# Token projections in spans of 512 tokens, queries with channels on partitions, row factors through memory

## The chip, the core and the metric

The kernel runs on one core of a Trainium2 chip. The metric is the device time of one execution in microseconds, the median of three runs. The engines are named as the profile names them: PE (matrix multiply) with PEld (its weight loads), DVE (vector), ACT (scalar), POOL (GpSimd) and SP, whose queue issues most transfers.

## The reference

One layer of a streaming encoder: 4096 prompt tokens and 32 sample tokens of 1024 channels. A row norm and one input projection of 3072 columns give queries, keys and values (512 each), a gate, a pooling input and its gate; then differential attention, trailing means, an output projection. The first sixteen channels of every 64 of a query or key are rotated by their position. Cut to what matters here:

```python
h = rmsnorm(x, norm_g)
proj = jnp.einsum('bsd,de->bse', h, w_in)
q, k, v, ga, u, gp = jnp.split(proj, [ATTN_WIDTH, 2 * ATTN_WIDTH, 3 * ATTN_WIDTH,
                                      4 * ATTN_WIDTH, 4 * ATTN_WIDTH + POOL_WIDTH], axis=-1)
q = rope(q.reshape(B, S, N_HEADS, 2, HEAD_DIM), pos)
k = rope(k.reshape(B, S, N_HEADS, 2, HEAD_DIM), pos)
k_rows, v_rows = k.reshape(B, S, N_HEADS, 128), v.reshape(B, S, N_HEADS, 128)    # outputs too
o = diff_attention(q, k_all.reshape(B, Lk, N_HEADS, 2, HEAD_DIM), v_all, pos, kpos_all, lam)
o = rmsnorm(o, subln_g, SUBLN_EPS) * (1.0 - lam_init)
a_out = o.reshape(B, S, ATTN_WIDTH) * jax.nn.silu(ga)
p_out = pool_mix(u, pool_hist, pos, w_pool, pool_scale) * jax.nn.silu(gp)
y = x + jnp.einsum('bse,ed->bsd', jnp.concatenate([a_out, p_out], axis=-1), w_out)
```

## The kernel before

The kernel has four stages: a token phase (queries, keys, values), a channel phase (gates and pooling), attention for four heads, and the output projection. Every product of the first two is made in three passes of rounded 32-bit numbers (`mm3`, L112 to L114): the high part of one operand with the high and the low part of the other, and its low part with the high part. A contraction over 1024 channels has eight chunks, so a sum takes 24 matmuls. `split` (L108, L109) makes the two parts: a rounded copy on ACT, the remainder on DVE.

The token phase goes over 33 blocks of 128 tokens (the last has 32). A block's transposed input is the stationary operand, and the weights, 1536 columns in two loads of 768, are the moving one. Four pieces of 512, 256, 256 and 512 columns fill three sums of 512: queries, keys, values. `evacuate` (L233, L235, L238) scales a row by the factor that `norms` has made of that token's norm (its square sum is L210); `rotate` turns queries and keys on POOL; `transposes` brings both across with eight PE transposes (L259), splits them and stores them in `q_scr` and `k_scr`, from which attention loads them. PE does a block's transposes after the next block's query sum.

The channel phase goes over nine spans (seven of 512 tokens, one of 256, one of 288), with the weights stationary and up to 512 tokens moving. `span_in` needs a token's factor in every partition: it multiplies an identity by the factors (`dg`, L349), and PE multiplies that by ones (`bps`, L350). `order` runs twelve sums a span; the last two spans' second halves are done in the attention phase.

A scheduler orders the instructions of each engine; each engine and each transfer queue works its list in order. Pools that bear on the change: `mid` (16 tiles of 4 KB a partition: split inputs, weights being converted), `st` (4: inputs as loaded), `sm` (8 of 2 KB: what comes out of a sum until its store has landed), `two` (three tiles of PSUM, each two banks, for the sums) and `one`, with a single bank for `tp`.

Of the kernel before, what the change touches and what calls it, by code (L numbers as in the profile page):

```python
# [30 lines left out]
LAM_INIT = 0.2  # L31
WINDOWS = (2, 4, 8, 16)
# [13 lines left out]
AFTER = {1: 12, 2: 15}  # L46
CSA = 7
# [21 lines left out]
def encoder(tc, a, o):  # L69
# [4 lines left out]
    with ExitStack() as es:  # L74
# [11 lines left out]
        q_scr = dram.tile([NH, 2, 2, 64, TOK], F32R, name="q_scr")  # L86
# [38 lines left out]
        latest, stages = [None], []  # L125
# [5 lines left out]
        def load_w(src, cols, scale, slot):  # L131

            width = sum(c1 - c0 for c0, c1 in cols)
            w = []
            for k in range(NK):
                if k % 2 == 0:
                    t = b_tile(slot + k // 2, [P, 2, 2, 768], "w")
                w.append((t[:, k % 2, 0], t[:, k % 2, 1]))
                stg = m_tile([P, 768], name="wst")
                stages.append(stg)  # L140
                x = 0
                for c0, c1 in cols:
                    dma(stg[:, x:x + c1 - c0], src[k * P:(k + 1) * P, c0:c1])
                    x += c1 - c0
                hi, lo = w[k][0][:, :width], w[k][1][:, :width]
                S.activation(hi, stg[:, :width], AF.Copy, scale=scale[:, k:k + 1])  # L146
                V.scalar_tensor_tensor(lo, stg[:, :width], scale[:, k:k + 1], hi.bitcast(F32),  # L147
                                       op0=ALU.mult, op1=ALU.subtract)
            return w
# [8 lines left out]
        ones = const.tile([P, P], F32, name="ones")  # L158
        rx = const.tile([P, NB + 1], F32, name="rx")
        rxq = const.tile([P, NB + 1], F32, name="rxq")  # L160
# [26 lines left out]


        def token_phase():

            pieces = [(0, 0, 512, 0, 0), (0, 512, 768, 1, 0), (1, 0, 256, 1, 256), (1, 256, 768, 2, 0)]

            def block_in(b):
                t0, m = b * P, (P if b < NB else DEC)
                xt = st.tile([P, NK, P], F32, tag="st", name="xt")
                if b in AFTER:
                    pace(xt[0:1, 0, 0:1], stages[AFTER[b]][0:1, 0:1])
                dma(xt[:, :, :m], a["xT"][:, t0:t0 + m].rearrange("(k p) t -> p k t", p=P))
                src = xt[:, :, :m]
                xh = m_tile([P, NK, P], F32R, name="xh")  # L200
                xl = m_tile([P, NK, P], F32R, name="xl")
                split(xh[:, :, :m], xl[:, :, :m], src)
                return [b, t0, m, xh, xl, None, [None] * 3]

            def norms(blk):
                b, t0, m = blk[:3]
                xn = m_tile([P, D], name="xn")
                dma(xn[:m], a["xn"][t0:t0 + m, :])
                junk = s_tile([P, D], BF16, name="junk")
                S.activation(junk[:m], xn[:m], AF.Square, accum_out=ss[:m, b:b + 1])  # L210
# [3 lines left out]
                V.tensor_scalar_mul(rxq[:m, b:b + 1], rx[:m, b:b + 1], 0.125)  # L214
                blk[5] = m_tile([P, D], name="qk")

            def accumulate(blk, ws, i, k):
                b, t0, m, xh, xl, qk, banks = blk
                wi, c0, c1, kind, x = pieces[i]
                if banks[kind] is None:  # L220
                    banks[kind] = p2_tile("ps")[:, 0:512]
                mm3(banks[kind][:m, x:x + c1 - c0], xh[:, k, :m], xl[:, k, :m], ws[wi][k][0][:, c0:c1],
                    ws[wi][k][1][:, c0:c1], k == 0, k == NK - 1)

            def project(blk, ws, i):
                for k in range(NK):
                    accumulate(blk, ws, i, k)

            def evacuate(blk, kind):
                b, t0, m, xh, xl, qk, banks = blk  # L230
                ps = banks[kind]
                if kind == 0:
                    V.tensor_scalar_mul(qk[:m, 0:512], ps[:m], rxq[:m, b:b + 1])  # L233
                elif kind == 1:
                    S.activation(qk[:m, 512:1024], ps[:m], AF.Copy, scale=rx[:m, b:b + 1])  # L235
                else:
                    v = s_tile([P, 512], name="v")
                    S.activation(v[:m], ps[:m], AF.Copy, scale=rx[:m, b:b + 1])  # L238
                    dma(o["v_prompt"][t0:t0 + m, :] if b < NB else o["v_sample"], v[:m])
                    dma(v_scr[:, :m, b].rearrange("h t e -> t h e"), v[:m].rearrange("t (h e) -> t h e", h=NH))  # L240

            def rotate(blk):
                b, t0, m, xh, xl, qk, banks = blk
                ab = qk[:m].rearrange("t (g d) -> t g d", d=64)[:, :, 0:16].rearrange("t g (z f) -> t g z f", z=2)
                rc = s_tile([P, 16, 2, 8], name="rc")
                rs = s_tile([P, 16, 2, 8], name="rs")
                bc = lambda i: cs[:m, b, i].unsqueeze(1).unsqueeze(1).to_broadcast([m, 16, 2, 8])
# [57 lines left out]
            for i, t in enumerate(tail):  # L305
                project(t, ws, 0)
                evacuate(t, 0)
                if i == 0:
                    transposes(blk)
# [772 lines left out]
```

## Time and profile before

| | |
|---|---|
| median of three runs | 2852.12 us (2845.03 to 2855.67) |
| profiled execution | 2851.88 us, span 2850.1 us, mean granted clock 0.996 |
| token phase, channel phase | to 593 us; first attention matmul at 1145.4 us |
| PE busy | 2791.5 us, 98% of the span |
| DVE, ACT, POOL busy | 1832.5, 1601.2, 277.3 us |
| transfers | 348.50 MB, mean 122 GB/s |

The profiled execution lies 0.24 us from the median, and 1.8 us of it lies outside the span. PE is counted as busy while matmuls overlap, so a full PE is not yet a PE at its fastest: the distance from one matmul's start to the next is what a matmul costs.

### The profile page before, as it was taken

How to read it: one execution, taken by the hardware profiler on the slowest of the kernel's cores; microseconds unless marked ns; L12 is line 12 of the kernel's file. 1: busy time of each engine (PE TensorE's matmuls, PEld its weight loads, DVE VectorE, ACT ScalarE, POOL GpSimd, SP SyncE). 2: the span in 40 equal slices, each digit the busy share in tenths (PEclk: the TensorE clock that was granted, in tenths of full speed). 3: DMA queues.
4: the chain of work that ended last, by engine and by line, in shares of the span. 5: the costliest groups of instructions: out<-in, count | busy, mean ns of one | idle time of the engine just before them, and what ended most of it. 6: DMA issues, size and time to landing. Idle time of an engine off the chain costs nothing. (4 is left out here: it accounts for less than half of the span.)

```text
span 2850.1 us, 44682 instructions
## 1 busy us (share of the span) xinstructions
PE 2791.5 (98%) x16637; PEld 2413.9 (85%) x16637; DVE 1832.5 (64%) x3565; ACT 1601.2 (56%) x3377; POOL 277.3 (10%) x511
## 2 busy tenths in 40 slices
PE   8999999999999999899999999999999989999999
PEld 7888888878888889788888788888888878888776
DVE  3222111265555555788888778788888888888666
ACT  4222222342222221478887787777888778888554
POOL 1111111110000011200001000011000110000000
PEclk9999999999999999999999999999999999999999
DMA  8555555562333344933327435356333451213883
GB/s 253 163 163 166 166 167 165 170 195 100 108 107 108 105 101 121 191 68 74 78 59 147 101 79 123 67 116 126 74 79 65 94 104 24 57 30 95 288 260 132
DMA packets 320009, 348.50 MB, mean 122 GB/s; under 512 B 26904, under 2 KB 250384, under 8 KB 319024
## 3 DMA queue, kind: packets, MB, share of 16 engines
q1 hardware_dynamic: 245184, 270.01, 30.7%
q0 software_dynamic: 74608, 75.64, 15.8%
q8 instruction: 131, 2.15, 0.3%
q14 instruction: 86, 0.70, 0.1%
HBM read 210.32 MB, written 135.26 MB: 121 GB/s over the span
## 5 line engine op out<-in xcount | busy, mean ns | idle before, releaser
L519 DVE TENSOR_REDUCE nm<-sc 128x1 f32<-128x1024 f32 (+8 forms) x612 | 637.0, 1046 | 110.4 <-PE sc L622 103.8
L622 PE MATMUL sc<-kv,qt 128*128 128x512 f32 (+2 forms) x2304 | 670.3, 404 | 19.1 <-ACT p L528 11.0
L650 PEld LDWEIGHTS av<-kv,at 128*128 128x128 f32 x4224 | 549.1, 191 | 32.7 <-DVE ot L656 2.7
L650 PE MATMUL av<-kv,at 128*128 128x128 f32 x4224 | 574.3, 275 | 1.6 <-DVE ot L656 1.3
L622 PEld LDWEIGHTS sc<-kv,qt 128*128 128x128 f32 x2304 | 391.0, 191 | 92.9 <-ACT p L528 36.5
L569 ACT COPY at<-tp 128x512 f32<-128x512 f32 (+3 forms) x579 | 318.6, 550 | 159.7 <-PE tp L566 156.4
L528 ACT ACTIVATE p<-sc,nm 128x1024 f32<-128x1024 f32 (+7 forms) x386 | 360.4, 935 | 68.8 <-DVE nm L519 64.3
L112 PE MATMUL ps<-w,xh 128*128 128x512 f32 (+3 forms) x1056 | 357.4, 340 | 8.9 <-ACT w L146 8.9
L113 PE MATMUL ps<-w,xh 128*128 128x512 f32 (+3 forms) x1056 | 356.1, 338 | 0.7 <-DVE w L147 0.6
L114 PE MATMUL ps<-w,xl 128*128 128x512 f32 (+3 forms) x1056 | 355.9, 337 | 0.2 <-DVE xl L109 0.2
L560 DVE SCALAR_TENSOR_TENSOR p<-p,c 128x1024 f32<-128x1024 f32 (+5 forms) x322 | 344.4, 1081 | 2.3
L566 PE MATMUL tp<-ident,p 128*128 128x128 f32 x2121 | 332.2, 274 | 4.2 <-ACT at L569 3.5
L112 PE MATMUL ps<-x,w 128*128 128x512 f32 (+2 forms) x864 | 318.6, 369 | 1.1 <-DVE u L392 1.1
L114 PE MATMUL ps<-x,w 128*128 128x512 f32 (+2 forms) x864 | 317.4, 367 | 0.0
L113 PE MATMUL ps<-x,w 128*128 128x512 f32 (+2 forms) x864 | 317.3, 367 | 0.0
L528 ACT ACTIVATE p<-sc,ref 128x1024 f32<-128x1024 f32 (+7 forms) x258 | 262.7, 1019 | 69.5 <-DVE ref L523 50.3
L566 PEld LDWEIGHTS tp<-ident,p 128*128 128x128 f32 x2121 | 251.0, 141 | 45.3 <-ACT at L569 19.1
L112 PE MATMUL yp<-wo,hl 128*128 128x512 f32 (+1 forms) x528 | 221.6, 420 | 11.7 <-DVE xn L897 6.0
L112 PEld LDWEIGHTS ps<-w,xh 128*128 128x128 f32 (+1 forms) x1056 | 198.1, 188 | 31.4 <-ACT w L146 9.4
L113 PEld LDWEIGHTS ps<-w,xh 128*128 128x128 f32 (+1 forms) x1056 | 198.5, 188 | 22.8 <-DVE w L147 2.1
L114 PEld LDWEIGHTS ps<-w,xl 128*128 128x128 f32 (+1 forms) x1056 | 198.3, 188 | 22.7 <-DVE xl L109 0.4
L113 PE MATMUL yp<-wo,hl 128*128 128x512 f32 (+1 forms) x528 | 208.7, 395 | 0.0
(155 smaller groups left out, 3381.3 us busy)
## 6 DMA issues: line engine op xcount, KB each, us to landing
xn<-xn SPq DMA_DIRECT2D x64, 512.0 KB, 3.9
qt<-q_scr POOLq DMA_DIRECT2D x128, 256.0 KB, 4.3
xt<-xT SPq DMA_DIRECT2D x32, 512.0 KB, 5.1
hl<-gp_scr POOLq DMA_DIRECT2D x32, 512.0 KB, 5.5
kv<-k_scr POOLq DMA_DIRECT2D x32, 512.0 KB, 9.9
x_scr<-xn SPq DMA_DIRECT2D x32, 512.0 KB, 5.3
xn<-x_scr SPq DMA_DIRECT2D x32, 512.0 KB, 4.5
y_prompt<-xn SPq DMA_DIRECT2D x32, 512.0 KB, 3.6
```

The source lines that it names most:

```text
L112: T.matmul(ps, lh, rh, start=first, stop=False)
L113: T.matmul(ps, lh, rl, start=False, stop=False)
L114: T.matmul(ps, ll, rh, start=False, stop=last)
L519: V.tensor_reduce(ref if self.ng == 1 and j else bias, sc, axis=AX.X, op=ALU.max, negate=True)
L528: S.activation(p[:, :w], sc, AF.Exp, bias=bias, accum_out=self.l[:, j, g:g + 1])
L560: V.scalar_tensor_tensor(p1[:, :w], p2[:, :w], self.c[:, g:g + 1], p1[:, :w], op0=ALU.mult, op1=ALU.add)
L566: T.transpose(tp[:blk.shape[1], i], blk, ident)
L569: S.copy(at[:r, :n], tp[:r, :n])
L622: T.matmul(sc[:, off:off + pw], qt[:, x, j, q0:q0 + P], keys[:, kk:kk + pw], start=x == 0, stop=x == 1)
L650: T.matmul(self.av[:, 0:P], self.at[:, i], self.value(kb), start=self.blk == 0, stop=self.blk == self.qb)
```

## The change

Queries, keys and values are now made in the same nine spans as the channel phase, and a span's split input serves all of them. A unit is one sum of 24 matmuls. A span of 512 has twelve: four of queries (128 channels on the partitions, weights stationary, 512 tokens moving: `q_sum`), four of keys and four of values (128 tokens stationary, all 512 columns moving: `project`). The query weights' columns are put in another order on the host, so that the first chunk of 128 holds all rotated pairs, first halves in partitions 0 to 63, second halves in 64 to 127. `q_out` scales by the factors along the free axis, rotates the first chunk with two copies that swap the halves (ACT) and three DVE operations with a table loaded per span, splits, and stores: no transposes. Keys are still transposed, four a block, after 18 matmuls of the next unit (`keys_across`), and are still rotated on POOL, by operations of half the old size.

A token's factors go to memory (`scales_out`, 4 bytes a token, into `rx_scr`) and come back in every partition (`scales`), in the token phase and in the channel phase; the `dg`, `bps` and `ones` are gone. `ahead` spreads the next span's loads, splits and norms over the units of the present one. The first span loads its weights in pieces of 512 columns and sums queries chunk by chunk while they arrive. Attention reads `q_scr` in another layout with as many rows of the same length; from its first matmul on, the order on PE and ACT is as before.

```diff
-        q_scr = dram.tile([NH, 2, 2, 64, TOK], F32R, name="q_scr")
+        q_scr = dram.tile([NH * 2, 2, 64, TOK], F32R, name="q_scr")
+        rx_scr = dram.tile([1, TOK], F32, name="rx_scr")
...
+        def scales(t0, n):
+
+            bc = s_tile([P, 512], name="bc")
+            dma(bc[:, :n], rx_scr[0:1, t0:t0 + n].to_broadcast([P, n]))
+            return bc
...
+            def scales_out(t0, n):
+                for t, m in blocks((t0, n)):
+                    dma(rx_scr[0:1, t:t + m].rearrange("o t -> t o"), rx[:m, t // P:t // P + 1])
...
+            def q_sum(ps, sp, i, k):
+                n, xh, xl = sp[1:4]
+                c = slice(i * P, (i + 1) * P)
+                mm3(ps[:, :n], w[0][k][0][:, c], w[0][k][1][:, c], xh[k][:, :n], xl[k][:, :n], k == 0, k == NK - 1)
+
+            def q_out(ps, sp, i, bc, tab):
+
+                t0, n = sp[:2]
+                z = s_tile([P, 512], name="z")
+                V.scalar_tensor_tensor(z[:, :n], ps[:, :n], 0.125, bc[:, :n], op0=ALU.mult, op1=ALU.mult)
+                if i == 0:
+                    zs = s_tile([P, 512], name="zs")
+                    S.copy(zs[0:64, :n], z[64:128, :n])
+                    S.copy(zs[64:128, :n], z[0:64, :n])
+                    V.tensor_mul(z[:, :n], z[:, :n], tab[:, 0, :n])
+                    V.tensor_mul(zs[:, :n], zs[:, :n], tab[:, 1, :n])
+                    V.tensor_add(z[:, :n], z[:, :n], zs[:, :n])
+                hi = s_tile([P, 512], F32R, name="hi")
+                lo = s_tile([P, 512], F32R, name="lo")
+                split(hi[:, :n], lo[:, :n], z[:, :n])
+                for l, t in ((0, hi), (1, lo)):
+                    for p0, p1, d in ((0, 64, 0), (64, 128, 8)) if i == 0 else ((0, P, i * 16),):
+                        dma(q_scr[:, l, d:d + (p1 - p0) // 8, t0:t0 + n].rearrange("g d t -> g d t").bitcast(F32),
+                            t[p0:p1, :n].bitcast(F32))
+
+            def project(ps, sp, t0, m, kind, k):
+                c = slice(t0 - sp[0], t0 - sp[0] + m)
+                xh, xl = sp[2:4]
+                mm3(ps[:m], xh[k][:, c], xl[k][:, c], w[kind][k][0], w[kind][k][1], k == 0, k == NK - 1)
...
+            def k_unit(sp, t):
+                ps = bank()
+                for k in range(NK):
+                    if k == 6:
+                        across()
+                    project(ps, sp, *t, 1, k)
+                held.append(keys_out(ps, *t))
...
+            def ahead(t0, n, first=0, step=2):
+
+                xh, xl, loads, splits = x_parts(t0, n)
+                sp = (t0, n, xh, xl, [])
+                jobs = {}
+                at = lambda u, f: jobs.setdefault(first + u, []).append(f)
+                xns = {}
+                for i, t in enumerate(blocks(sp)):
+                    def into(i=i, t=t):
+                        xns[i] = norm_in(*t)
+                    at(step * i, into)
+                    at(step * i + 2, lambda i=i, t=t: norm(*t, xns[i]))
+                for c, (load, cut) in enumerate(zip(loads, splits)):
+                    at(step * c + step - 1, load)
+                    at(step * c + step + 1, cut)
+                at(step * 3 + 3, lambda: scales_out(t0, n))
+                at(step * 3 + 4, lambda: sp[4].extend([scales(t0, n), table(t0, n)]))
+                return sp, jobs
...
+            for k in range(NK):
+                load_piece(0, k)
+                xt, h_, l_ = [t[:, k % 2] for t in xs[k // 2]]
+                dma(xt, a["xT"][k * P:(k + 1) * P, t0:t0 + n])
+                split(h_, l_, xt)
+                xh.append(h_)
+                xl.append(l_)
+                for i in range(4):
+                    q_sum(qb[i], sp, i, k)
...
+            def rest():
+                extra.extend([scales(t0, n), table(t0, n)])
+                for i in range(4):
+                    q_out(raw[i], sp, i, *extra)
+
+            nxt, jobs = ahead(*SPANS[1], 1, 1)
+            jobs[1].insert(0, rest)
+            run([lambda t=t: k_unit(sp, t) for t in bl[2:]] + [lambda t=t: v_unit(sp, t) for t in bl], jobs)
+            for s in range(1, len(SPANS) - 2):
+                sp = nxt
+                nxt, jobs = ahead(*SPANS[s + 1])
...
+                run([lambda i=i: q_unit(sp, i) for i in range(4)] + [lambda t=t: k_unit(sp, t) for t in bl] +
+                    [lambda t=t: v_unit(sp, t) for t in bl], jobs, jobs2)
...
             def span_in(t0, n):
-                bc = s_tile([P, 512], name="bc")
-                bps = p1_tile("av", "bps")
-                for i in range((n + P - 1) // P):
-                    m = min(P, n - i * P)
-                    b = t0 // P + i
-                    dg = etiny.tile([P, P], F32, name="dg")
-                    V.tensor_scalar_mul(dg[:m, :m], ident[:m, :m], rx[:m, b:b + 1])
-                    T.matmul(bps[:, i * P:i * P + m], ones[:m, :], dg[:m, :m], start=True, stop=True)
-                S.copy(bc[:, :n], bps[:, :n])
...
+                bc = scales(t0, n)
+                return (t0, n, bc) + x_in(t0, n)
```

The first place is PE in the middle of the token phase. Before, the end of a block's query sum (`ps_924`), the eight transposes of the block before it, and the first of the pieces of 256 columns (`ps_978`):

```order
L112 MATMUL ps_924<-w_140,xh_825 128x512
L113 MATMUL ps_924<-w_140,xh_825 128x512
L114 MATMUL ps_924<-w_140,xl_826 128x512
L259 MATMUL tp_950<-ident_91,qk_745 128x128 x4
L259 MATMUL tp_961<-ident_91,qk_745 128x128 x4
L112 MATMUL ps_978<-w_113,xh_825 128x256
L113 MATMUL ps_978<-w_113,xh_825 128x256
L114 MATMUL ps_978<-w_113,xl_826 128x256
```

Now, the 18th matmul of a key unit (`ps_1462`), the four key transposes of the block before it, and the unit going on:

```order
L112 MATMUL ps_1462<-w_292,x_971 128x512
L113 MATMUL ps_1462<-w_292,x_971 128x512
L114 MATMUL ps_1462<-w_292,x_972 128x512
L314 MATMUL tp_1481<-ident_92,kt_1448 128x128 x4
L112 MATMUL ps_1462<-w_292,x_1071 128x512
L113 MATMUL ps_1462<-w_292,x_1071 128x512
L114 MATMUL ps_1462<-w_292,x_1072 128x512
```

The query transposes are gone from the row, the key transposes moved from between two sums into a sum, and the width after them is 512.

The second place is ACT. Before, one block: input split, the two halves brought across, keys out, norm, values out:

```order
L108 CAST xh_1123<-xt_1121 128x1024
L108 CAST hi_1104<-tp_1099 128x512
L108 CAST hi_1115<-tp_1110 128x512
L235 ACTIVATE qk_1043<-ps_1127,rx_100 128x512
L210 ACTIVATE junk_1186,ss_102<-xn_1184 128x1024
L213 ACTIVATE rx_100<-ss_102 128x1
L238 ACTIVATE v_1218<-ps_1193,rx_100 128x512
```

Now, the first span, from the swap copies of its first query chunk (`zs_506`) to the copy that empties the fourth key unit (`kt_586` from `ps_550`):

```order
L278 COPY zs_506<-z_504 64x512
L279 COPY zs_506<-z_504 64x512
L108 CAST x_649<-x_648 128x1024
L252 ACTIVATE xn_685,ss_101<-xn_685 128x1024
L108 CAST hi_512<-z_504 128x512
L255 ACTIVATE rx_100<-ss_101 128x1
L108 CAST hi_522<-z_520 128x512
L108 CAST x_690<-x_689 128x1024
L108 CAST hi_530<-z_528 128x512
L108 CAST hi_538<-z_536 128x512
L108 CAST hi_574<-tp_569 128x512
L299 ACTIVATE kt_586<-ps_550,rx_100 128x512
```

The copy that frees a PSUM tile stands at the end of twelve instructions, of which the first two wait for `z_504`, made on DVE from the factors `bc_500`.

The third place is SP's queue at the same point of the first span, from the first key blocks' stores to the load of the fourth norm input of the second span:

```order
L308 DMA k_prompt<-kt_429 128x512
L205 DMA x_596<-xT 128x2x512
L308 DMA k_prompt<-kt_437 128x512
L247 DMA xn_644<-xn 128x1024
L319 DMA k_scr_77<-hi_469 128x4x128
L319 DMA k_scr_77<-lo_470 128x4x128
L319 DMA k_scr_77<-hi_480 128x4x128
L319 DMA k_scr_77<-lo_481 128x4x128
L308 DMA k_prompt<-kt_492 128x512
L221 DMA bc_500<-rx_scr_76 128x512
L205 DMA x_648<-xT 128x2x512
L247 DMA xn_685<-xn 128x1024
```

The load of the factors (`bc_500`) stands behind the store of `kt_492`, which waits for POOL's rotation of that block; before, there was no such load.

## Rows read from the trace of the kernel before

**Rows 1.** Page, busy time of each engine.
```profile
PE 2791.5 (98%) x16637; PEld 2413.9 (85%) x16637; DVE 1832.5 (64%) x3565; ACT 1601.2 (56%) x3377; POOL 277.3 (10%) x511
```

**Rows 2.** Windows: stretch, then busy (instructions) per engine, clock, DMA share, GB/s.
```profile
100.00:150.00 50.00, 50.00 (x302) 44.62 (x301) 10.21 (x19) 13.70 (x23) 5.58 (x10) 1.00 0.58 171
...
700.00:750.00 50.00, 50.00 (x222) 41.30 (x221) 33.26 (x47) 14.17 (x20) 6.24 (x4) 1.00 0.36 122
```

**Rows 3.** Timeline of DVE: start us, length us, instruction; each block's query copy.
```profile
53.84 0.75 DVE L233 TENSOR_SCALAR qk<-ps,rxq 128x512 f32<-128x512 f32 x1 [8.32 <-PE ps L114]
...
544.96 0.75 DVE L233 TENSOR_SCALAR qk<-ps,rxq 128x512 f32<-128x512 f32 x1 [8.32 <-PE ps L114]
```

**Rows 4.** Timeline of PE in one token block.
```profile
557.76 0.39 PE L113 MATMUL ps<-w,xh 128*128 128x512 f32 x1
...
562.06 0.39 PE L114 MATMUL ps<-w,xl 128*128 128x512 f32 x1
562.29 1.03 PE L259 MATMUL tp<-ident,qk 128*128 128x128 f32 x8
...
563.52 0.28 PE L112 MATMUL ps<-w,xh 128*128 128x256 f32 x1
...
565.92 0.28 PE L114 MATMUL ps<-w,xl 128*128 128x256 f32 x1
```

**Rows 5.** Timeline of PE, 288 moving columns in the channel phase.
```profile
1104.13 0.30 PE L112 MATMUL ps<-x,w 128*128 128x288 f32 x1
...
1106.66 0.29 PE L113 MATMUL ps<-x,w 128*128 128x288 f32 x1
```

**Rows 6.** Timeline of PE around a span's factors, then its waits, 560 to 700.
```profile
688.91 0.61 PE L350 MATMUL bps<-dg,ones 128*128 128x128 f32 x4
...
690.05 0.71 PE L350 MATMUL bps<-dg,ones 128*128 128x128 f32 x4
...
691.30 0.39 PE L112 MATMUL ps<-x,w 128*128 128x512 f32 x1
...
PE bps L350 <- DVE dg L349: 2.6, 1, 2.6
PE tp L259 <- POOL qk L251: 0.9, 1, 0.9
```

**Rows 7.** Timelines of PE and ACT at the start, and windows there.
```profile
8.38 1.01 PE L112 MATMUL ps<-w,xh 128*128 128x512 f32 x2 [8.38 <-ACT w L146]
...
12.80 0.45 PE L112 MATMUL ps<-w,xh 128*128 128x512 f32 x1
...
0.73 1.28 ACT L108 ACT_TABLE_LOAD   x1 [0.73 <-PEq L1074]
...
2.00:4.00 2.00, 0.00 (x0) 0.00 (x0) 0.00 (x0) 0.02 (x1) 0.00 (x0) 1.00 0.69 174
4.00:6.00 2.00, 0.00 (x0) 0.00 (x0) 0.00 (x0) 0.43 (x1) 0.00 (x0) 1.00 1.08 269
```

**Rows 8.** Groups by line and form, 100 to 500: busy us, mean ns of one.
```profile
L210 ACT ACTIVATE junk<-xn 128x1024 bf16<-128x1024 f32 x23 | 24.1, 1048 | 0.0
L108 ACT CAST xh<-xt 128x1024 fp32r<-128x1024 f32 x23 | 23.9, 1039 | 0.0
...
L248 POOL TENSOR_TENSOR rc<-qk,cs 128x256 f32<-128x256 f32 x23 | 17.1, 742 | 348.4 <-ACT qk L235 348.4
...
L235 ACT ACTIVATE qk<-ps,rx 128x512 f32<-128x512 f32 x23 | 15.9, 689 | 118.0 <-PE ps L114 118.0
...
L251 POOL TENSOR_TENSOR qk<-rc,rs 128x128 f32<-128x128 f32 x22 | 10.1, 459 | 0.0
```

**Rows 9.** DMA issues, 100 to 500, then 0 to 40: KB, median us to landing.
```profile
q_scr<-hi SPq DMA_DIRECT2D x23, 256.0 KB, 2.3
...
q_scr<-lo SPq DMA_DIRECT2D x1, 256.0 KB, 5.0
...
sub<-outcol SPq DMA_DIRECT2D x1, 2.5 KB, 3.4
```

More of the change, by code (lines that the diff above doesn't have):

```diff
@@ L31 @@
 LAM_INIT = 0.2
+SPANS = [(i * 512, 512) for i in range(7)] + [(3584, 256), (3840, 288)]
 WINDOWS = (2, 4, 8, 16)
@@ new lines, in run @@
+            def run(units, *jobs):
+                for u, unit in enumerate(units):
+                    for j in jobs:
+                        for f in j.pop(u, []):
+                            f()
+                    unit()
+                for j in jobs:
+                    for u in sorted(j):
+                        for f in j[u]:
+                            f()
+            t0, n = SPANS[0]
+            xh, xl = [], []
+            xs = [[p.tile([P, 2, 512], d, tag=g, name="x") for p, d, g in ((st, F32, "st"), (mid, F32R, "m"), (mid, F32R, "m"))]
+                  for _ in range(4)]
@@ L319, in token_phase @@
[L319 to L322 removed]
+            raw = []
+            for x in range(2):
+                r = m_tile([P, 2, 512], name="raw")
+                for i in range(2):
+                    S.copy(r[:, i], qb[x * 2 + i])
+                    raw.append(r[:, i])
+            both = p2_tile("ps")
+            for k in range(NK):
+                for i in range(2):
+                    project(both[:, i * 512:i * 512 + 512], sp, *bl[i], 1, k)
@@ new lines, in token_phase @@
+            for t, xn in zip(bl, xns):
+                norm(*t, xn)
+            scales_out(t0, n)
+            for k in range(NK):
+                load_piece(2, k)
+            for i in range(2):
+                held.append(keys_out(both[:, i * 512:i * 512 + 512], *bl[i]))
+            def rest():
[4 more added lines that the diff above has]
+            jobs[1].insert(0, rest)
@@ new lines, in token_phase @@
+            lam_in()
+            sps = [nxt, last]
+            todo = [(sp, t) for sp in sps for t in blocks(sp)]
+            w2, load2, convert2 = load_w(a["w_in"], [(1536, 2048), (2048, 2176), (2560, 2688)], gcol, 0)
+            jobs = {8 + k // 2: [] for k in range(0, NK, 2)}
+            jobs[0], jobs[2] = [third[0]], [third[1]]
+            for k in range(NK):
+                jobs[8 + k // 2].append(lambda k=k: load2(k))
+            jobs[11] += [lambda k=k: convert2(k) for k in range(4)]
@@ new lines, in token_phase @@
+            jobs[13] = [lambda k=k: convert2(k) for k in range(4, NK)]
+            jobs[14] = [lambda: next(channel)]
+            run([lambda sp=sp, i=i: q_unit(sp, i) for sp in sps for i in range(4)] +
+                [lambda sp=sp, t=t: k_unit(sp, t) for sp, t in todo] + [lambda sp=sp, t=t: v_unit(sp, t) for sp, t in todo], jobs)
+            w3, load3, convert3 = load_w(a["w_in"], [(2176, 2560), (2688, 3072)], gcol, 4)
+            for k in range(NK):
+                load3(k)
+                convert3(k)
@@ L326, in channel_phase @@
+            return [w2, w3]
         def channel_phase():
```

289 lines of the change are left out of this document (139 added, 150 removed).

## Prediction

> **What bounds the kernel now.** I read the page's busy times first: PE is busy 98% of the span [rows 1], but that counts overlapping matmuls. The windows show that in the two stages that the change touches PE never stops while DVE and ACT work less than two thirds of the time, and transfers take a little over half of their engines' time at most [rows 2]. So a microsecond of PE work removed there is a microsecond of the whole, as long as nothing else becomes late; attention and output, whose order does not change, follow as they are. The distance between matmul starts gives the price of PE work. Nineteen steps of 512 columns take 4.30 us, 0.2265 us each; twenty of 256 take 2.40 us, 0.120 each [rows 4]; nineteen of 288 take 2.53 us, 0.133 each [rows 5]. Eight transposes and three matmuls of 256 take 1.23 us, so the transposes and the change to and fro cost 0.87 [rows 4]. A block is then 48 x 0.2265 + 48 x 0.120 + 0.87 = 17.50 us; from the 28 periods between two query copies I get 17.54 [rows 3]. That agreement is what makes the sum worth trusting: PE waits for nothing inside a block.
>
> **Token phase, steady part.** Before: 33 blocks x 17.54 = 578.8 us, the block of 32 tokens too, since its moving side is as wide. After: seven spans of twelve units and ten key and value units of the last two spans, 94 units of 24 x 0.2265 = 5.44, make 511.0. The last two spans' queries move only 256 and 288 columns: 96 x (0.120 + 0.133) = 24.3. Key transposes stay, four a block: half of the eight, plus the change to and fro, some 0.48, x 33 = 15.8. Sum 551.1, so **27.7 us** less: about 13 from query transposes, 11 from taking 512 columns where two halves stood, 3 from the short last spans.
>
> **Factors through memory.** The identity products leave PE. Two groups of them and six other matmuls take 2.39 us, so the groups cost 2.39 - 6 x 0.2265 = 1.03 [rows 6]; 33 products at four to such a pair make 8.25 x 1.03 = 8.5. The wait of 2.6 us for the scaled identity and the 0.9 us for the last block's rotation, which stood at the end of the token phase, go too [rows 6]. Together **12.0 us**. What comes instead is a store of four bytes a token and a load of 256 KB, neither in the trace. A store of such short rows (2.5 KB) landed in 3.4 us, a load or store of 256 KB in 2.3, in the crowded start 5.0 [rows 9]; the two in sequence are bounded by 4 and 9 us. In order of the queue they stand about a dozen transfers, some two units of 5.44 us, before the first query copy that needs them, and three PSUM tiles let PE run two units further. I take nothing for them, and 9 us a span if that cover were gone.
>
> **What becomes late next.** DVE gains per span four copies from PSUM with two inputs, three more operations for the first chunk, and loses little; at 10.2 busy of 50 us [rows 2] it has room. Key transposes stand 18 matmuls, 4.08 us, into the next unit. Until then ACT must empty the sum (0.69) and POOL rotate in four operations; the rotated half now has 128 and 64 columns where it had 256 and 128. These cost between 4 x 0.46 and 2 x 0.74 + 2 x 0.46 [rows 8], so 2.5 to 3.1 us in all: late by nothing, with 1 us to spare. I put 2 us for the hand-overs between spans and stages together (below nothing is excluded, since each is only a wait).
>
> **The start.** Before, the first matmul starts at 8.38, and the twelve until 12.80 (six of each width) take 4.42 us where later ones take 2.08 [rows 7], a loss of 2.3. Two blocks and a query sum, less a block's transposes, are 2 x 17.54 + 5.44 - 0.87 = 39.65 us of work, and the copy after them is at 53.84 [rows 3]: 14.1 us lost in all. After, the first sum needs 0.52 MB instead of 0.9: by the first two windows [rows 7] that lands at about 4.6; ACT loads its table behind the weights' landing (1.28 us), converts weights and input, and PE starts near 6.4. With the same slow stretch 8.7 us are lost. From then on a chunk is twelve matmuls, 2.7 us, for 0.5 MB, and PE stays fed. But the first span's queries are parked and finished late: PE reaches the fifth unit after the query sums (the third of values) near 65 us, and it needs the tile of the fourth key block, emptied by ACT at the end of the twelve instructions that the change section shows. They wait for the factors, and these for SP behind a store that waits for POOL: the third key unit ends near 48, its rotation near 52, the factors land 2.3 to 5.0 us later [rows 9], and the twelve take 0.7 to 1.05 us each for the large ones [rows 8], some 8, with gaps for DVE 11. So the tile is free at 66 to 68, the transposes behind it 2 us later: 3 to 8 us of waiting, bounds 0 and 10; I take 5. Loss 13.7 against 14.1: **0.4 us** gained.
>
> **Sum.** 27.7 + 12.0 + 0.4 - 2 = 38.1 us. The profiled execution took 2851.9, as the median did (2852.1), so **2814 us**.
>
> The Trainium skill has a rule against the second share of the 27.7: "TensorE: Matmul & The Clock Gate", section "Back-to-back issue gap", gives a warm gap of N/2.4 + 2.5 ns, so 109 ns for 256 columns and 216 for 512: two halves would cost only 2.5 ns more than a whole, and 33 x 24 merged pairs would give 2 us instead of 11. The trace disagrees: 0.120 and 0.2265.
>
> **Rivals.**
> *Merging pays nothing.* If the 512-wide key and value units run at twice the cost of the 256-wide ones, because their weight loads (one per matmul) and not their columns set the pace, 10.7 us are not gained: 2824.5. Against it: both widths were measured in the same blocks with the same loads [rows 4]. 3%.
>
> *The transfer queue holds the spans up.* Transfers hand over worse than assumed: every span waits once for a landing in the crowded way, 5.0 instead of 2.3 us [rows 9], seven times 2.7 = 19 us: 2833. For it: ACT and DVE now have waits for `sm` tiles whose query stores must have landed, and one queue in order carries a short-row store, its reload and 20 large transfers a span. Against it: steps between need and supply of two units. 15%. The skill's "DMA: Bandwidth & Descriptors", section "Why a DMA increments its semaphore by 16 and not by 1", lets a transfer use the largest number up to 16 that divides both slowest dimensions: the new query stores, eight groups of rows, would run on 8 engines instead of 16. No run here shows it yet.
>
> *The start is longer or shorter.* At its bounds the wait of 5 us is 0 or 10, the first matmul may be 2 us off: 2807 to 2821, inside the range.
>
> *Slower.* ACT works in order, and a norm's square (1.05 us) and a cast (1.04) [rows 8] can stand ahead of each key copy. Both ahead: 2.5 to 3.1 becomes 4.6 to 5.2, so 0.5 to 1.1 us late at each of 33 transposes. It eats all of the gain from 38/33 = 1.2 us late at each, and makes the kernel slower by 0.5% from (38 + 14)/33 = 1.6; if the squares also wait for their input, 2.2 us late each, it gives 2887. Against it: in the order one square, no cast stands ahead of most key copies. 4%.
>
> *The change doesn't do what it says.* If query units with stationary weights ran slower than the trace's channel sums, the gain would show there; 222 instructions in 50 us of the channel phase [rows 2], at 0.2265 each, leave no room. 1%.
>
> **How the numbers follow.** The forecast has 70%, and its own range, from the start's bounds and 0 to 6 us for hand-overs, is 2806 to 2822. Better than that, if also no wait at the start and none at hand-overs comes, 7%; merging 3%, the queue 15%, slower 4%, no effect 1%. The range that leaves out at most two in ten reaches from 2804 to 2832. What this kernel's measurement can tell from no change is 0.5%, 14 us. Faster by more than that (below 2837.9) come the forecast, better, merging, and nine tenths of the queue: 0.93; within it 0.03; slower 0.04.
>
> **What would show it.** Right: matmul starts 0.2265 apart in all units of a full span, a span every 12 x 5.44 + 1.9 = 67.2 us against 4 x 17.54 = 70.2; no identity products; first channel sum near 566 instead of 593; the first attention matmul 38 us earlier than 1145.4, and equal distances after it. A wait of PE of some 5 us between 60 and 75 us, released by ACT. Wrong: PE waiting for POOL or ACT before the key transposes in every unit; PE waiting for DVE's query copies, these for the factors; query stores that land in over 5 us; a slower granted clock in the token phase; attention starting early and ending at the old time.

## The result, and the profile after

The changed kernel takes 2867.52 us (median of four runs, 2865.25 to 2871.01), the kernel before 2850.53 on the same chip: a ratio of 1.0061, with a 95% interval of 1.0039 to 1.0083. It is 17 us slower, where 2814 us and 38 us of gain were forecast. The profiled execution took 2871.01 us, its span is 2869.2.

The page's busy times are almost those of before [rows 1]; they don't show what happened:

```profile
PE 2769.3 (97%) x15719; PEld 2361.0 (82%) x15719; DVE 1839.7 (64%) x3543; ACT 1615.5 (56%) x3403; POOL 247.4 (9%) x507
```

Two marks in PE's timeline, with the end of the span, place it: the first channel sum and the first attention matmul, first in the changed kernel, then in the kernel before.

```profile
625.17 0.39 PE L112 MATMUL ps<-x,w 128*128 128x512 f32 x1
...
1164.38 1.08 PE L750 MATMUL sc<-kv,qt 128*128 128x512 f32 x4
...
592.92 0.47 PE L112 MATMUL ps<-x,w 128*128 128x512 f32 x1
...
1145.39 1.08 PE L622 MATMUL sc<-kv,qt 128*128 128x512 f32 x4
```

The first channel sum starts at 625.17 us instead of 592.92: the token phase became 32 us longer, where 27 less were expected. From there to the first attention matmul (1164.4, before 1145.4) it is 539.2 us instead of 552.5: the channel phase gained 13.3, where 12.0 was the forecast. Behind that mark nothing changed, 19.0 us late there and 19.1 at the end. So one stage, the token phase, came out otherwise than forecast, by some 59 us. PE's waits up to 640 us (total, times, longest):

```profile
PE tp L314 <- POOL kt L307: 37.7, 7, 16.3
PE ps L112 <- ACT kt L299: 10.3, 1, 10.3
PE ps L112 <- ACT x L108: 6.5, 1, 6.5
PE tp L314 <- DVE lo L109: 0.2, 1, 0.2
```

The third is the start of the kernel. The others, 48.2 us, are new. PE's timeline shows where they stand (in brackets the wait and who ended it), and those of ACT and SP show what was late around the longest:

```profile
54.47 1.11 PE L314 MATMUL tp<-ident,kt 128*128 128x128 f32 x4 [8.76 <-POOL kt L307]
...
85.90 0.79 PE L112 MATMUL ps<-w,x 128*128 128x512 f32 x1 [10.31 <-ACT kt L299]
...
148.20 1.12 PE L314 MATMUL tp<-ident,kt 128*128 128x128 f32 x4 [16.27 <-POOL kt L307]
...
222.68 1.12 PE L314 MATMUL tp<-ident,kt 128*128 128x128 f32 x4 [4.77 <-POOL kt L307]
...
438.50 0.66 PE L314 MATMUL tp<-ident,kt 128*128 128x128 f32 x4 [1.86 <-POOL kt L307]
...
134.57 1.04 ACT L108 CAST x<-x 128x1024 fp32r<-128x1024 f32 x1 [10.15 <-DMA x<-xT]
...
144.81 1.06 ACT L252 ACTIVATE xn<-xn 128x1024 f32<-128x1024 f32 x1 [6.68 <-DMA xn<-xn]
...
145.86 0.67 ACT L299 ACTIVATE kt<-ps,rx 128x512 f32<-128x512 f32 x1
...
123.52 0.47 SPq L205 DMA_DIRECT2D x<-xT  x1
...
126.80 3.38 SPq L259 DMA_DIRECT2D rx_scr<-rx  x4
...
134.63 0.59 SPq L247 DMA_DIRECT2D xn<-xn  x1
```

The reading: PE waits for transposes of the first key block of a span. Its copy (L299) stands on ACT behind a square (L252), that behind a cast (L108), and each of these waits for a landing. The input issued at 123.52 had not landed before 134.5, the rows issued at 134.63 not before 144.8: 10 to 11 us for 512 KB. Once POOL has the copy it rotates in time. Between the two loads SP issues two query stores, then four stores of factors (the row shown) and the load of a table. The windows show what transfers did around such stores (four issued from 126.80 to 130.18, a single one at 408.78), and what else it cost:

```profile
100.00:150.00 50.00, 33.73 (x148) 27.70 (x147) 13.10 (x26) 15.81 (x29) 1.46 (x4) 0.86 0.79 183
150.00:200.00 50.00, 50.00 (x221) 41.24 (x220) 11.49 (x23) 16.04 (x26) 4.43 (x12) 0.97 0.90 187
...
126.00:129.50 3.50, 3.50 (x18) 2.88 (x16) 0.00 (x0) 0.00 (x0) 0.00 (x0) 1.00 0.57 172
129.50:134.50 5.00, 2.42 (x11) 1.69 (x9) 0.00 (x0) 0.00 (x0) 0.00 (x0) 1.00 0.77 81
408.00:411.00 3.00, 3.00 (x15) 2.49 (x14) 0.32 (x2) 0.58 (x4) 0.00 (x0) 1.00 1.04 356
412.50:417.50 5.00, 5.00 (x24) 4.14 (x23) 3.15 (x5) 1.23 (x2) 0.00 (x0) 1.00 0.89 94
...
438.00:446.00 8.00, 7.50 (x28) 6.13 (x29) 0.69 (x1) 1.28 (x2) 1.91 (x6) 0.79 1.01 160
```

The last two columns are the share of the transfer engines' time and GB/s. Behind the four stores the rate is half of what it was while they were issued (81 after 172); some 4 us behind the single one it is a quarter (94 after 356). Yet the engines show a share of 0.77 and 0.89: there is no lack of transfers, packets are under way and finish late. Before, 0.58 went with 171 GB/s on average [rows 2]. The 40 slices of the stretch from 129.5 to 134.5, 0.125 us each, show it plainly:

```profile
DMA  5655585555948499909000000060100003090500
GB/s 197 214 197 197 213 180 213 181 165 181 182 148 164 164 115 115 49 33 49 0 0 0 0 0 16 33 16 0 16 0 16 16 0 33 16 16 0 66 33 16
DMA packets 413, 0.41 MB, mean 81 GB/s; under 512 B 215, under 2 KB 215, under 8 KB 413
```

After two microseconds at mostly 150 to 214 GB/s next to nothing lands, for three. Half of this stretch's packets are small ones.

### The profile page after: what moved, and what is told of

Same layout as the page of the kernel before. It is cut to its first block, busy times and chain, and to the rows that moved or that the text cites. A ratio compares the mean times of both kernels' runs of the same rounds, so it can differ in the third digit from the quotient of the medians.

```text
span 2869.2 us, 42987 instructions
## 1 busy us (share of the span) xinstructions
PE 2769.3 (97%) x15719; PEld 2361.0 (82%) x15719; DVE 1839.7 (64%) x3543; ACT 1615.5 (56%) x3403; POOL 247.4 (9%) x507
## 5 line engine op out<-in xcount | busy, mean ns | idle before, releaser
L112 PE MATMUL ps<-x,w 128*128 128x512 f32 (+2 forms) x1152 | 423.7, 368 | 7.6 <-ACT x L108 6.5
L113 PE MATMUL ps<-x,w 128*128 128x512 f32 (+2 forms) x1152 | 423.4, 368 | 0.0
L114 PE MATMUL ps<-x,w 128*128 128x512 f32 (+2 forms) x1152 | 423.3, 367 | 0.1
L694 PEld LDWEIGHTS tp<-ident,p 128*128 128x128 f32 x2121 | 251.0, 141 | 45.2 <-ACT at L697 19.1
L112 PEld LDWEIGHTS ps<-x,w 128*128 128x128 f32 x1152 | 217.0, 188 | 43.8 <-ACT x L108 6.5
L113 PEld LDWEIGHTS ps<-x,w 128*128 128x128 f32 x1152 | 217.1, 188 | 36.0 <-DVE x L109 0.4
L114 PEld LDWEIGHTS ps<-x,w 128*128 128x128 f32 x1152 | 217.1, 188 | 35.7 <-DVE w L239 0.5
L112 PE MATMUL ps<-w,x 128*128 128x512 f32 (+1 forms) x528 | 214.2, 406 | 10.3 <-ACT kt L299 10.3
L113 PE MATMUL ps<-w,x 128*128 128x512 f32 (+1 forms) x528 | 210.6, 399 | 0.0
L114 PE MATMUL ps<-w,x 128*128 128x512 f32 (+1 forms) x528 | 210.4, 398 | 0.0
```

Source lines behind the costliest of these rows:

```text
L112: T.matmul(ps, lh, rh, start=first, stop=False)
L113: T.matmul(ps, lh, rl, start=False, stop=False)
L114: T.matmul(ps, ll, rh, start=False, stop=last)
L694: T.transpose(tp[:blk.shape[1], i], blk, ident)
```

## The experiments

There were three explanations at first. Theory A: ACT's order puts work that waits for loads ahead of the key copy. Theory B, its rival in the first expectation: the transfers are late, whoever waits for them. Theory D: the loads are late because they stand in one queue behind query stores. Theory E: these stores are slow. Whether POOL could empty the key sums in ACT's place, the plainest test of theory A, has no measurement. All times below are to be held against 2867.5 us for the changed kernel and 2850 to 2851 for the kernel before.

**1. Squares and casts one unit later.** In the spans after the first, `late` puts a job behind the unit instead of ahead of it; the stores of factors move with them.

```diff
-                    at(step * i + 2, lambda i=i, t=t: norm(*t, xns[i]))
+                    at(step * i + 2 + late, lambda i=i, t=t: norm(*t, xns[i]))
...
-                    at(step * c + step + 1, cut)
+                    at(step * c + step + 1 + late, cut)
```

> In the spans after the first, squares and casts of the next span's input are written behind the unit in whose place they stood, so one key copy comes ahead of each square. Theory A: the four waits of 1.9 to 4.8 us (222, 295, 367, 438 us) vanish with their slow matmuls, 21 us, and the one of 16.3 at 148 us falls to some 4, since a cast that waits for its load until 134.6 still stands ahead of that key copy (unit done near 131): 2867.5 - 21 - 13 = 2833, 2828 to 2845. Theory B (transfers late whoever waits): a gain under 10 us.

Measured: 2874.09 us (2870.77 to 2883.0), no gain. The 7 us more are not clear of noise: 1.0088 of the kernel before (1.0066 to 1.0109), against 1.0061 (1.0039 to 1.0083). The waits for POOL became ten of 51.5 us in all, the longest 21.6. With four `st` tiles a later square also frees its tile later, so that the load behind it can start later; that this is what kept the gain away was not tried. Theory A alone is out; theory B, a gain under 10 us, is left standing.

**2. The loads of the next span on POOL's queue** (table and factors too, in lines not shown).

```diff
-                xh, xl, loads, splits = x_parts(t0, n)
+                xh, xl, loads, splits = x_parts(t0, n, rdma)
...
-                        xns[i] = norm_in(*t)
+                        xns[i] = norm_in(*t, rdma)
```

> The loads of the next span (rows for the norm, transposed input, table, factors) are issued by POOL's queue instead of SP's, so they do not stand behind query stores that wait for ACT; the order on ACT stays. Theory A in its simple form (too much work ahead of the key copy, loads late by bandwidth): the waits from 148 us on stay within a third, 2855 or more. Theory D (a loop: the load is issued behind a store, the store waits for a cast on ACT, the cast stands behind a square that waits for the load before): the waits from 148 us on vanish, 28 us and some 13 of slow clock, 2820 to 2835; the two at 54 and 86 us stay.

Measured: 2945.91 us (2945.47 to 2961.72), 78 us slower than the changed kernel. POOL's waits from 100 to 600 us, and its timeline before one transpose:

```profile
POOL rot L304 <- ACT kt L299: 113.5, 21, 18.9
POOL xn L247 <- DVE x L109: 99.6, 8, 17.4
POOL x L205 <- DVE ss L253: 77.2, 5, 17.2
...
343.16 0.70 POOL L205 DMA_DIRECT2D x<-xT  x1 [16.40 <-DVE ss L253]
346.02 0.45 POOL L304 TENSOR_TENSOR rot<-kt,cs 128x128 f32<-128x128 f32 x1 [2.15 <-ACT kt L299]
```

The issue of a load waits for a free tile (`DVE ss` is the norm whose square frees it), and now the rotation stands behind that issue. Loads were not held by SP's stores alone; the edit put a second wait ahead of the rotation. It speaks against the simple loop of theory D, but mixes two things, and I drew no more from it.

**3. Each query chunk stored in one piece.**

```diff
-        q_scr = dram.tile([NH * 2, 2, 64, TOK], F32R, name="q_scr")
+        q_scr = dram.tile([64, NH * 2, 2, TOK], F32R, name="q_scr")
...
-                    for p0, p1, d in ((0, 64, 0), (64, 128, 8)) if i == 0 else ((0, P, i * 16),):
-                        dma(q_scr[:, l, d:d + (p1 - p0) // 8, t0:t0 + n].rearrange("g d t -> g d t").bitcast(F32),
-                            t[p0:p1, :n].bitcast(F32))
+                    dma(q_scr[i * 16:(i + 1) * 16, :, l, t0:t0 + n].rearrange("d g t -> (d g) t").bitcast(F32),
+                        t[:, :n].bitcast(F32))
...
-    perm = np.concatenate([col[:, 0:8].ravel(), col[:, 8:16].ravel()] + [col[:, d:d + 16].ravel() for d in (16, 32, 48)])
+    perm = col.T.ravel()
```

> Query channels are ordered so that each chunk's store is one piece of 128 rows, a destination whose slowest dimension is 128 rows instead of eight groups (8 stores a span instead of 10). Theory E (query stores that run on half of the engines fill the queue and make the loads land 7 to 11 us after their issue): the waits from 148 us on fall by more than half, 2845 or less. Theories A and D: the stores are only one link, under 10 us: 2857 to 2868.

Measured: 2886.01 us (2881.06 to 2894.85), 18 us slower, clear of noise (1.0104 to 1.0154 of the kernel before) and outside what either theory allowed; PE's waits behind the start grew from 48.2 to 59.9 us. So storing in eight groups was not what made the loads late. From 100 to 150 us the query stores of this version took 10.9 and 11.6 us to land (`hi`, `lo`), and the stores of factors beside them 15.1.

None of the theories about order, queue or query stores had held, so I went back to the slices shown above. The stretch without bytes begins some 1.3 us behind the issue of the last store of factors, each of which is 128 pieces of 4 bytes. That gave theory F: these stores clog memory for whatever is under way with them.

**4. The factors stored as rows.** PE transposes the span's columns of factors, so that a store has pieces of 512 bytes.

```diff
-                for t, m in blocks((t0, n)):
-                    dma(rx_scr[0:1, t:t + m].rearrange("o t -> t o"), rx[:m, t // P:t // P + 1])
+                nb, m, b = n // P, n % P, t0 // P
+                ps = p1_tile("av", "rps")
+                row = etiny.tile([4, P], F32, name="row")
+                T.transpose(ps[:nb, :P], rx[:, b:b + nb], ident)
+                V.tensor_copy(row[:nb], ps[:nb, :P])
+                dma(rx_scr[0, t0:t0 + nb * P].rearrange("(b p) -> b p", p=P), row[:nb])
...
```

> The factors of a span reach memory as rows: PE transposes the span's columns of factors (128 by 4), DVE copies them and one store of 512 bytes a row takes the place of four stores of 128 pieces of 4 bytes. Theory F (the stores of 4 bytes clog memory: in the changed kernel the transfers run at 172 to 356 GB/s up to such a store and at 81 to 123 in the 5 us behind it, while engines show busy): loads land in time again, the waits from 148 us on (28.5 us, and some 12 of slow matmuls) vanish, those at 54 and 86 us (19.6, and 5) shrink by up to a half: 2815 to 2828. Theory G (ring: four tiles for eight loads a span, each freed only by the square or cast that ACT does in order, so loads are late whatever memory does): the waits stay, 2860 or more.

Measured: 2832.45 us (2831.04 to 2836.16), 35 us faster than the changed kernel and 0.9938 of the kernel before (0.9920 to 0.9957). PE's waits to 600 us:

```profile
PE tp L324 <- POOL kt L317: 9.4, 7, 3.9
PE ps L112 <- ACT kt L309: 8.4, 1, 8.4
PE ps L112 <- ACT x L108: 6.9, 1, 6.9
PE ps L112 <- DVE z L285: 1.9, 1, 1.9
PE tp L324 <- DVE lo L109: 0.4, 1, 0.4
```

Against 48.2 us there are 20.1 left behind the start, and the longest wait for POOL falls from 16.3 to 3.9. Theory F's mechanism holds; the time is 4 us above its range. The waits up to 90 us shrank from 19.6 to 11.4 in all, as it allowed (the one of 10.3 only to 8.4), but those further on did not vanish: 8.6 of 28.5 us are left, 3.9 of them at 126 and 1.9 at 136. Theory G (the ring of four tiles) would have left the waits.

**5. The same, and the old stores beside it.**

```diff
+                for t, c in blocks((t0, n)):
+                    dma(junk_scr[0:1, t:t + c].rearrange("o t -> t o"), rx[:c, t // P:t // P + 1])
```

> As the factor rows, and beside them the old stores of 4 bytes go to a place that nobody reads, so nothing waits for their data. Theory F: the waits and the slow transfers are back, 2855 to 2875. Theory H (it was the hand-over, that the queue waits for the factors' landing before it reads them back, not the stores' form): as the factor rows alone, within 8 us of it.

Measured: 2895.25 us (2889.63 to 2900.89), 63 us more, with waits for POOL of 49.7 us in ten pieces. Nothing reads these stores, so it is not the hand-over (theory H) but the stores themselves. It is 20 us above the range that I gave; why both kinds together cost more than the old one alone is not settled.

**6. The old stores in the kernel before.** One line behind `rxq` in `norms`, read by nobody.

```diff
+                dma(junk_scr[0:1, t0:t0 + m].rearrange("o t -> t o"), rx[:m, b:b + 1])
```

> The kernel before, and after each block's norm a store of its factors in pieces of 4 bytes, to a place that nobody reads: the disputed cost by itself. Theory F: in the 5 us behind a store transfers run under 130 GB/s with engines shown busy, and landings of loads (3.7 and 5.0 us in the median between 200 and 250 us) become longer by 2 to 5 us; a block of 17.5 us has the slack to hide it, so the time stays within 0.5%, 2848 to 2862. Theory H: landings as before.

Measured: 2867.38 us (2866.8 to 2869.09), 1.0059 of the kernel before (1.0044 to 1.0073). I had expected the block's slack to hide it; it did not at the start (a wait of 6.2 us for weights at 29 us) and at the stage's end (5.0 instead of none at 588). These two places account for 10.8 of the 16.4 us; in the blocks between them PE has no new wait, so there the slack did hide it. The transfers themselves, 200 to 250 us, with KB and median us to landing, first two lines of the kernel before, then this version's:

```profile
xt<-xT SPq DMA_DIRECT2D x3, 512.0 KB, 5.0
xn<-xn SPq DMA_DIRECT2D x3, 512.0 KB, 3.7
...
xt<-xT SPq DMA_DIRECT2D x3, 512.0 KB, 7.3
xn<-xn SPq DMA_DIRECT2D x2, 512.0 KB, 9.1
q_scr<-hi SPq DMA_DIRECT2D x3, 256.0 KB, 5.4
...
junk_scr<-rx SPq DMA_DIRECT2D x3, 0.5 KB, 9.5
```

A store of half a kilobyte takes 9.5 us, and the others are late with it: query stores that landed in 2.3 us [rows 9] take 5.4, the rows for the norm 9.1 instead of 3.7.

**7. The old stores in the kernel before, 512 bytes apart.**

```diff
+        junk_scr = dram.tile([TOK, P], F32, name="junk_scr")
...
+                dma(junk_scr[t0:t0 + m, 0:1], rx[:m, b:b + 1])
```

> The kernel before with the store of 128 pieces of 4 bytes a block as measured (16.4 us slower), but each piece 512 bytes from the next instead of beside it. Theory K (neighbouring pieces fall into the same stretch of memory and are written one after another): transfers run on at 200 GB/s and more behind the store, and the time is that of before, 2848 to 2855. Theory L (any 128 pieces of 4 bytes clog, wherever they go): slow stretches as measured, 2862 to 2872.

Measured: 2851.91 us (2846.93 to 2856.26, ten runs), 0.9996 of the kernel before (0.9982 to 1.0010). The same view:

```profile
xt<-xT SPq DMA_DIRECT2D x3, 512.0 KB, 5.9
xn<-xn SPq DMA_DIRECT2D x3, 512.0 KB, 4.0
...
q_scr<-hi SPq DMA_DIRECT2D x3, 256.0 KB, 2.3
junk_scr<-rx SPq DMA_DIRECT2D x3, 0.5 KB, 1.9
```

As many pieces of the same size, from the same tile, in the same place of the queue, now land in 1.9 us. In these 50 us the profile counts 848 packets under 512 B, 840 in experiment 6 and 402 in the kernel before. So it is neither the size nor the number of pieces but that they are neighbours in memory (theory K). Only the distances of 4 and 512 bytes were measured. What happens inside the memory, no view here shows.

The rest are versions on top of the factor rows, to see whether the forecast's other terms were sound.

**8. Factor rows, squares and casts one unit later** (the edits of 4 and 1).

> Factor rows, and squares and casts of the spans after the first are written behind the unit in whose place they stood. With factor rows alone (2832.5 us) PE still waits 3.9 and 1.9 us at 126 and 136 us for key copies that stand on ACT behind a square waiting 8.0 us for its rows, and 0.8 at 402. Theory A (ACT's order is what is left): these vanish, 6.6 us and some 3 of slow matmuls, 2821 to 2827. Theory G (a ring of four tiles: a later square frees its tile later, so the next load comes later): no gain, 2830 to 2842, as the same edit alone cost 7 us.

Measured: 2835.9 us (2833.19 to 2837.99): no gain, as theory G had it; that the ring of tiles is the reason was not tried by itself.

**9. Factor rows, the first span's queries ended piece by piece.**

```diff
-            jobs[1].insert(0, rest)
+            q_end = lambda i: q_out(raw[i], sp, i, *extra)
+            jobs[0] = [lambda: extra.extend([scales(t0, n), table(t0, n)])]
+            jobs[2].insert(0, lambda: q_end(0))
+            jobs[3][:0] = [lambda: q_end(1), lambda: q_end(2)]
+            jobs[4].insert(0, lambda: q_end(3))
```

> Factor rows, and the end of the first span's queries is not in one piece ahead of the fourth key block but a chunk, two, and one ahead of the first three value blocks; factors and table are loaded a unit earlier. Theory: the wait of 8.4 us at 76 us (the fourth key block's copy behind those twelve instructions on ACT, the step that the prediction put at 5) and the 0.7 behind it vanish with 3 us of slow matmuls: 2832.5 - 12 = 2820, 2817 to 2826. Rival: the casts then stand ahead of the value copies and the next span's squares, the wait moves there, and less than 5 us is gained.

Measured: 2827.36 us (2825.94 to 2833.41), 5 us less instead of 12, and not clear of noise in the whole time (0.9882 to 0.9927 of the kernel before, against 0.9920 to 0.9957 for factor rows alone). In the profiled executions the first channel sum starts 8.6 us earlier (581.9 instead of 590.5). The 8.4 us at 76 us are gone, but a wait further on grew:

```profile
118.46 1.06 ACT L252 ACTIVATE xn<-xn 128x1024 f32<-128x1024 f32 x1 [8.24 <-DMA xn<-xn]
...
121.84 1.12 PE L324 MATMUL tp<-ident,kt 128*128 128x128 f32 x4 [7.56 <-POOL kt L317]
```

It is the chain of theory A, a square that waits for its rows ahead of the key copy. In experiment 4 the same square waited until 122.4; PE now reaches these transposes 8.2 us earlier (114.3 instead of 122.5), the rows only 3.9. The queries that now end later bring their stores nearer to these loads, which may be why the rows did not come earlier too; that was not tried by itself.

**10. Factor rows, query chunks in one piece** (the edits of 4 and 3).

> Factor rows, with each query chunk stored in one piece. Alone this edit made the kernel 18 us slower, where nothing or a gain was expected. Theory I (its stores use more engines at a time and so ran harder into the transfers that the stores of 4 bytes held up): with the factor rows the loss is gone, within 4 us of 2832.5. Theory J (the layout itself is slow to write, 33 KB from row to row instead of 16.5): query stores land later here too, and 10 to 20 us are lost again, 2842 to 2852.

Measured: 2826.97 us (2819.46 to 2831.37), 5.5 us less than factor rows alone, again not clear of noise (0.9869 to 0.9923); the first channel sum starts 10.2 us earlier (580.3). The edit that cost 18 us beside the old stores costs nothing without them, and its query stores `hi` land in 2.9 us from 100 to 150, where those of experiment 3 took 10.9. So it is not the layout (theory J). Why it lost so much beside them (theory I) was not tried further.

**11 and 12. Edits 4, 9 and 3 together, and with the later squares as well.**

> Three edits together: factor rows, the first span's queries ended a chunk or two at a time, one store for each query chunk. Alone on factor rows (2832.5 us) the second gave 5 us and the third 5.5. What stood in the way of the second was a new wait of 7.6 us at 122 us, where a key copy stands on ACT behind a square that waits 8.2 us for its rows; with one-piece stores that wait was 2.9. Theory A: the gains add and the wait at 122 falls to 3 or less, 2814 to 2820. Rival: the end of the queries, moved later, presses the stores and loads of the next span together whatever the stores' form, the 7.6 stays: 2821 to 2826.

> The three edits, and squares and casts of the spans after the first behind the unit in whose place they stood. Theory A: the wait left at 122 us vanishes, 2 to 5 us less than the three edits alone. Theory G (each later square frees its tile later and the next load starts later): the same within 2 us, or up to 5 us slower, as on the changed kernel (7 us) and on factor rows (3.5 us).

Measured: 2814.22 us (2809.96 to 2822.17), 0.9877 of the kernel before (0.9857 to 0.9897), and 2812.81 us (2811.53 to 2815.22), 0.9868 (0.9852 to 0.9883). The two don't differ by more than they spread. So theory A holds for the first (the gains add, and no wait for POOL is longer than 1.6 us) and theory G for the second. In the first, PE's waits to 600 us, and DVE's copy of the first query sum of three spans:

```profile
PE ps L112 <- ACT x L108: 6.5, 1, 6.5
PE tp L323 <- POOL kt L316: 2.8, 4, 1.6
PE ps L112 <- DVE z L285: 1.8, 1, 1.8
...
222.36 0.68 DVE L285 SCALAR_TENSOR_TENSOR z<-ps,bc 128x512 f32<-128x512 f32 x1
...
289.58 0.68 DVE L285 SCALAR_TENSOR_TENSOR z<-ps,bc 128x512 f32<-128x512 f32 x1
...
356.83 0.68 DVE L285 SCALAR_TENSOR_TENSOR z<-ps,bc 128x512 f32<-128x512 f32 x1
```

## Why the prediction was wrong

**The step that failed.** "What comes instead is a store of four bytes a token and a load of 256 KB, neither in the trace", and, at its end, "I take nothing for them". I bounded the store by a landing of short rows (3.4 us; the prediction calls it a store, in the kernel it is a load, into `sub`) and by those of large transfers [rows 9], and then asked only when the factors themselves would be there. Both were wrong: such a store lands in 9.5 us when it alone is added to the kernel before, and its real price is what it does to the transfers beside it. As those were loads on which ACT's order hangs, four stores a span made PE wait. Stored as rows, the factors cost 35 us less: PE's waits behind the start fall from 48.2 to 20.1 us, and with them most of the slow matmuls behind them; the first channel sum starts at 590.5 instead of 625.2 us.

**A second step, smaller.** With factor rows the kernel is still 18 us above the forecast. PE then waits 20.1 us behind the start, where the sum had 5 for the fourth key block and 2 for hand-overs, and nothing for matmuls at a lower clock behind a wait. Edits 9 and 3, which leave the factors alone, take 18 us more together. With edits 4, 9 and 3 the channel phase starts at 568.4 us with 4.7 us of waits behind the start, in the changed kernel at 625.2 with 48.2. Of the 56.8 us between them 43.5 are waits; the other 13.3 I put down to slower matmuls, as the granted clock over the first 600 us is 0.95 in the changed kernel and 1.00 with the three edits.

**Token phase, 27.7 us: right where PE does not wait.** Between the DVE copies shown above, of the kernel with the three edits, lie 67.22 and 67.25 us a span; 67.2 was forecast. The rival "merging pays nothing" would have needed more than that: 8 key and value units at twice the 0.120 of [rows 4] are 2.6 us longer a span. The rival "the change doesn't do what it says" falls with it.

**Factors, 12.0 us: right on PE's side.** The channel phase is 13.3 us shorter in the changed kernel. What PE gave up there came back in the stage ahead, by transfers.

**The start, 0.4 us: wrong, in one part foreseen.** The first matmul starts at 6.50 (forecast 6.4). The wait of 5 us for the fourth key block is 10.3, at 76 to 86 us instead of between 60 and 75; with factor rows it is 8.4, with the end of the queries spread it is gone. A wait of 8.8 us at 54 was not in the sum at all: the first key copies stand on ACT behind the casts of the value weights, which landed at 44 and 51 us. With factor rows 0.7 us of it remain, so most of it was the stores.

**The rivals.** "Slower" named the chain that decided, a square waiting for its input ahead of the key copy, POOL's rotation, transposes that wait. I gave it 4%, because in the order one square stood ahead of most key copies; the order was right, but I put its inputs down as landed, and priced the other case (2887 us) without a chance of its own. It needed only one key copy to be late in each of five spans, by 1.9 to 16.3 us, not every one by 1.6. "The transfer queue holds the spans up" named the short-row store among the queue's load, but priced the crowding at 2.7 us a span, 2833 us in all. It drew on the Trainium skill, "DMA: Bandwidth & Descriptors", section "Why a DMA increments its semaphore by 16 and not by 1": a destination with eight groups outermost would use 8 engines. A store with 128 rows outermost took 5.5 us less with factor rows, within noise, and lost 18 without them; no run shows how many engines either used.

**The sum.** The change with its stores mended takes 2832.5 us, not 2814. That the kernel with two more edits takes 2814.2, its first attention matmul 37.7 us ahead of that of before (1107.7 against 1145.4; 38 in the forecast), is in part luck: those edits also took away waits that the sum had counted in, 5 us at the start among them. What it does show is that PE's own work was priced rightly. The range, made of the start's bounds and of hand-overs, left out that a new transfer can harm others than itself.

## What to carry to other kernels

A column of 4-byte values, one a partition, cost this kernel 35 us when it was stored to neighbouring addresses: transpose it first and store rows, or leave distance between the pieces (512 bytes were enough here). An operation that the trace of before doesn't show should be measured alone beside the traffic that it will meet; its bytes don't tell what it does to others. And where a load's consumer stands on an in-order engine ahead of the copy that feeds PE, what the load is late beyond the slack of that copy is PE's: ACT's waits for two loads, 10.2 and 6.7 us, became one of 16.3 on PE.

## What the runs showed of the hardware

Stores of 128 neighbouring pieces of 4 bytes took 9.5 us to land in the kernel before, and what was beside them landed later (256 KB in 5.4 us instead of 2.3); 512 bytes apart they took 1.9 us. Behind such stores the transfer engines showed a share of 0.77 and 0.89 with 81 and 94 GB/s, so there a high share next to a low rate marked a stall and not a load.

A wait of PE can cost more than itself. Behind one of 1.86 us at 438.5 the stretch to 446 shows a granted clock of 0.79 in the mean of its two levels, 2.4 and 1.2 GHz. Yet a wait of 2.6 us of the kernel before [rows 6], at 621 us, was followed by full clock, and so was one of 1.8 us at 498 with the three edits; what decides between them no run shows. Over the changed kernel's token phase this added some 13 us, by the difference worked out above, to 43.5 of waiting.
